# All 31 taps of the depthwise convolution of both channel halves on VectorE

## The chip, the cores and the metric

One NeuronCore of a Trainium2 chip. The metric is the device time of one launch in microseconds (us), the median of the timed runs. Engines are named as in the profile: PE is TensorE (matrix products and transposes), PEld its weight loads, DVE is VectorE, ACT is ScalarE, POOL is GpSimd.

## What is computed

Two layers of a first block and two layers of a second block run over 256 tokens of width 1024, in float32. The part that the change touches is a branch of the first block's mixer: 512 columns of a projection, gated to 256 channels, go through a causal depthwise convolution over 31 tokens, a layer norm, a SiLU and a small product.

```python
CONV_WIDTH, CONV_KERNEL = 256, 31

def conformer_conv(u, conv_dw, conv_b, ln_g, ln_b, conv_pw):
    a, g = jnp.split(u, 2, axis=-1)
    y = a * jax.nn.sigmoid(g)
    y = lax.conv_general_dilated(
        y, conv_dw[:, None, :], window_strides=(1,), padding=[(CONV_KERNEL - 1, 0)],
        dimension_numbers=('NWC', 'WIO', 'NWC'), feature_group_count=CONV_WIDTH)
    y = y + conv_b
    y = jax.nn.silu(layernorm(y, ln_g, ln_b))
    return jnp.einsum('bsc,cd->bsd', y, conv_pw)

# in each of the two layers of the first block:
#   y_attn = sparse attention (index scores, 64 best keys, softmax), 512 columns
#   y_conv = conformer_conv(...), 256 columns; y_pool = windowed means, 256 columns
#   h += rmsnorm(concat(y_attn, y_conv, y_pool) @ w_out); then feed forward and gate
```

## The kernel before

The 256 tokens are two halves of 128 (`t` = 0 and 1). Both halves run the same program, written as two generators; the second is held `LAG` = 4 steps behind the first, and each step is one load of weights: two planes of 128 rows by up to 512 columns (`cols`, line 115, or `rows`, line 137). The weights are loaded once and used by both halves. Each load is split exactly into two parts (`weights`, line 88): ScalarE rounds it to the high part (`whi`, line 101), VectorE subtracts to get the low part (`wlo`, line 102). Nine such pairs are kept (`SLOTS`). With inputs split in the same way, a product is three matmuls (`mm3`, lines 111 to 113): high by high, high by low, low by high. One load serves six matmuls for each half of the tokens. Sums go to two PSUM banks tagged `mm`, which ScalarE empties (`evac`, line 176); that step is moved forward in the scheduler's order by `URGENT`.

Small work that follows a product (transposes, rotary embedding at lines 395, 397 and 574, index scores at lines 584 to 592, selection of keys at lines 600 and 601, softmax) is hung behind later loads as chains of steps (`after`, `tick`). A scheduler then sets the order on each engine, once and for all: of the instructions that it takes to be ready, the one written first in the program goes first.

The convolution has channels on partitions: `conv_in[j]` holds channels 128 j to 128 j + 127 of all 256 tokens, with 30 zero columns ahead. When the second half of the tokens has filled it (`local_fill`), `pool_all` (the windowed means, lines 700 to 707, on VectorE) and `conv_all` are written. In `conv_all`, tap 0 with the bias is a ScalarE activation (line 729). Of channels 0 to 127, taps 1 to 26 are 26 ScalarE copies scaled by the tap (`part`, line 732, two buffers) that GpSimd adds up one after the other (line 733); taps 27 to 30 are summed on VectorE in `mine` (lines 745 and 747) and added by GpSimd (line 749). Of channels 128 to 255, taps 1 to 30 are 30 multiply-adds on VectorE (line 740), each of which reads the sum that the one before it wrote. `conv_finish` follows much later, ahead of the part of `w_out` that reads it.

Of the kernel before, what the change touches and what calls it, by code (L numbers as in the profile page):

```python
# [26 lines left out]
MP = 3  # L27
POOL_TAPS = (27, 1)
PARTS = 2
# [16 lines left out]
class Net:  # L46
# [15 lines left out]

# [1 line left out]
    def tile(self, shape, tag, dtype=F32, bufs=2, pool=None):  # L64
        return (pool or self.wk).tile(shape, dtype, tag=tag, name=tag, bufs=bufs)

    def mid(self, *shape):
        """A tile of up to 528 columns, shaped."""
        n = int(np.prod(shape))
        o = self.wk.tile([P, 528], F32, tag="mid", name="mid", bufs=MID)[:, :n]  # L70
        return o if len(shape) == 1 else self.shaped(o, shape)

    def small(self, *shape):
        """A tile of up to 320 columns, shaped."""
        n = int(np.prod(shape))
        o = self.wk.tile([P, 320], F32, tag="small", name="small", bufs=SMALL)[:, :n]
        return o if len(shape) == 1 else self.shaped(o, shape)
# [8 lines left out]

# [1 line left out]
    def weights(self, t, load):  # L88
        """The next two planes of weights in program order, [128, 2, width], as (hi, lo)."""
        i = self.pos[t]  # L90
        self.pos[t] += 1
        if t == 1:
            return self.cache.pop(i)
        nc = self.nc
        raw = self.raw_p.tile([P, 2, 512], F32, tag="raw", name="raw", bufs=RAW)
        hi = self.w_p.tile([P, 2, 512], F32R, tag="whi", name="whi", bufs=SLOTS)
        lo = self.w_p.tile([P, 2, 512], F32R, tag="wlo", name="wlo", bufs=SLOTS)
        width = load(raw)
        src = raw[:, :, :width]
        with self.tc.issue_after(self.last_act.ins) if i == 0 else nullcontext():  # L100
            nc.scalar.activation(hi[:, :, :width], src, AF.Copy)  # L101
        nc.vector.tensor_sub(lo[:, :, :width], src, hi[:, :, :width].bitcast(F32))  # L102
        self.cache[i] = hi, lo
        return hi, lo
# [10 lines left out]
    def cols(self, t, lhs, w, pieces, ps, ks=range(KD), first=True, last=True):  # L115
        """ps = x @ w[:, pieces], the pieces side by side; ks the rows' tiles."""
        ks = list(ks)
        width = sum(n for _, n in pieces)
        for c in range(0, len(ks), 2):
            k0 = ks[c]  # L120
# [16 lines left out]
    def rows(self, t, lhs, w, row0, nk, accs, first, last):  # L137
        """accs (two halves of 1024 columns) += x @ w[row0:row0 + 128 nk]."""
        for c in range(nk):
# [11 lines left out]

# [1 line left out]
    def after(self, t, steps, side=0):  # L153
# [17 lines left out]

# [1 line left out]
    def evac(self, out, ps, func, **k):  # L173
        """Empties a bank of products, before what the scheduler has pending."""
        with self.tc.high_priority(URGENT):
            self.nc.scalar.activation(out, ps, func, **k)  # L176
# [4 lines left out]
    def split(self, dst, k0, n, src):  # L181
        """src [128, 128 n] exactly as hi + lo at tiles k0.."""
        hi, lo = (d[:, k0:k0 + n, :] for d in dst)
        src = src.rearrange("p (k c) -> p k c", k=n)
        self.nc.scalar.activation(hi, src, AF.Copy)  # L185
        self.nc.vector.tensor_sub(lo, src, hi.bitcast(F32))
# [5 lines left out]
    def turn(self, dst, k0, n, src):  # L192
        """Tiles k0.. of dst = the transposed 128-column blocks of src, split."""
        ps = self.bank("tr")
        for j in range(n):
            self.transpose(ps, j, src[:, j * P:(j + 1) * P])
        self.split(dst, k0, n, ps[:, :n * P])
# [5 lines left out]
    def turn_scaled(self, src, vec, c0):  # L203
        """(src * vec)^T split, vec along the features."""
        nc = self.nc
# [14 lines left out]
    def rsqrt(self, sums, n, eps, half=False):  # L220
        """(sums / n + eps) ** -0.5 of one or several columns, or half of it; sums: the parts
        of the sums."""
        g = self.nc.gpsimd
# [54 lines left out]

# [1 line left out]
    def setup(self):  # L280
# [36 lines left out]
    def setup_late(self):  # L317
        nc, cp = self.nc, self.cp
        # in the room of what only the first block needed
        room = lambda tag, n: self.shaped(self.tile([P, n], tag, bufs=1)[:, :SEQ], (2, P))  # L320
# [8 lines left out]
        for l in range(2):  # L329
# [7 lines left out]
            nc.scalar.activation(e, e, AF.Exp)  # L337
            # ln(1 + e) with the rounding of 1 + e made good
            nc.vector.tensor_scalar(q, e, 1.0, None, op0=ALU.add)
# [17 lines left out]
    def rope_table(self, pos, freq, n, tag):  # L357
        """(cos, sin) of pos * freq, the angle brought to [-pi, pi] in three exact steps."""
        nc, cp = self.nc, self.cp
# [30 lines left out]
    def turned(self, a, b, x, table, n):  # L390
        """a = x cos, b = (second half, first half of x) (-sin, sin), in each of n heads."""
        v = self.nc.vector
# [5 lines left out]

# [1 line left out]
    def block1(self, t, l):  # L400
# [30 lines left out]

        # index queries and keys first, then the queries of the attention itself
        S = (t + 1) * P
# [91 lines left out]

        # feed forward
        x, r = self.pre_norm(t, vec, 8)
# [17 lines left out]

        # gate
        pe = self.small(256)
# [21 lines left out]
    def rotate(self, t, u, n):  # L569
        """Rotary embedding of the first 16 of every 64 columns, in place."""  # L570
        x = u.rearrange("p (h s d) -> p h s d", s=8, d=8)[:, :, 0:2, :]
# [4 lines left out]
    def score_index(self, t, jj, wi, qiT, kiT, idx, first):  # L576
        """idx += relu(qi ki) wi for the heads 4 jj .. 4 jj + 3."""
        nc = self.nc
# [16 lines left out]
    def select(self, t, idx):  # L595
        """idx = 0 at the 64 largest of those that may be seen, far below elsewhere."""
        nc = self.nc
# [63 lines left out]
    def local_start(self, t, l):  # L661
        """Room and weights for the convolution and the pool, of both halves of the tokens."""
        nc, io = self.nc, self.io
# [24 lines left out]
    def pool_all(self):  # L688
        """Windowed means less the input; the first 16 tokens see fewer."""
        v = self.nc.vector  # L690
# [31 lines left out]
    def conv_all(self, l):  # L722
        """Some of the taps on the vector engine, the others on the scalar engine and the Pool."""
        nc, vec = self.nc, self.v1[l]
# [59 lines left out]

# [1 line left out]
    def swiglu(self, t, l, name, c0):  # L786
# [27 lines left out]
    def gated(self, t, x, hr, w, name, accs, mix, then=None):  # L814
        """mix += (1 + tanh(gate / 2)) accs; the half of it comes at the end."""
        nc = self.nc
# [13 lines left out]
    def history(self, t, key, buf, n):  # L830
        """The n columns before buf's own: the other half's last, or none."""
        if t == 0:
# [5 lines left out]
    def features(self, s, nk, buf, k0, n):  # L838
        """buf[:, k0:k0 + nk, n:] = s^T."""
        tr = self.bank("tr")  # L840
# [5 lines left out]
    def mixer(self, t, l):  # L846
# [7 lines left out]

        # the recurrent branch's inputs between the heads of the retention
        ha, mix = [], []
# [54 lines left out]

        # short convolution
        bufs = [self.mid(4, 2 + P) for _ in range(2)]
# [59 lines left out]
    def block_diagonal(self, t, l, n, j):  # L973
        """Four 128-blocks, each of two 64-blocks of the gates' weights."""
        def make():
# [8 lines left out]
    def lru(self, t, l, j, s, out):  # L984
        """512 channels of the recurrent branch, twice over, appended to out."""
        nc = self.nc
# [30 lines left out]
        v = nc.vector  # L1017
        # half of log(a); a by its eighth root; 1 - a^2 = -tanh(log(a)) (1 + a^2)
        v.scalar_tensor_tensor(a, a, 1.0, lam[:, :, None].to_broadcast([P, 4, P]), op0=ALU.add, op1=ALU.mult)
# [63 lines left out]

# [1 line left out]
    def program(self, t, layers):  # L1085
# [46 lines left out]

# [1 line left out]
_BIG = ["w_in", "conv_pw", "pool_w", "w_out", "norm_mix_post", "w_up", "w_down", "norm_mlp_post",  # L1134
# [57 lines left out]
```

## Time and profile before

| | us |
|---|---|
| median of 3 timed runs | 2426.82 (2425.52 to 2427.87) |
| span of the profiled execution | 2426.7 |
| TensorE busy | 2361.9 |
| VectorE busy | 1570.9 |
| ScalarE busy | 1377.2 |
| GpSimd busy | 114.6 |

The two convolutions lie at about 50 to 90 us and 411 to 452 us of the span. A timeline row gives the start and the duration of an instruction, its engine, line and operation, what it writes and reads, and in brackets how long its engine stood still before it and what ended that. Instructions of an engine overlap a little: the step from one start to the next is what counts for its throughput. A windows row gives, for one stretch, the busy time of each engine with its instructions, the clock granted to TensorE as a share of 2.4 GHz, and the DMA traffic.

### The profile page before, as it was taken

How to read it: one execution, taken by the hardware profiler on the slowest of the kernel's cores; microseconds unless marked ns; L12 is line 12 of the kernel's file. 1: busy time of each engine (PE TensorE's matmuls, PEld its weight loads, DVE VectorE, ACT ScalarE, POOL GpSimd, SP SyncE). 2: the span in 40 equal slices, each digit the busy share in tenths (PEclk: the TensorE clock that was granted, in tenths of full speed). 3: DMA queues.
4: the chain of work that ended last, by engine and by line, in shares of the span. 5: the costliest groups of instructions: out<-in, count | busy, mean ns of one | idle time of the engine just before them, and what ended most of it. 6: DMA issues, size and time to landing. Idle time of an engine off the chain costs nothing.

```text
span 2426.7 us, 30886 instructions
## 1 busy us (share of the span) xinstructions
PE 2361.9 (97%) x10912; PEld 1913.5 (79%) x10912; DVE 1570.9 (65%) x2460; ACT 1377.2 (57%) x2137; POOL 114.6 (5%) x212
## 2 busy tenths in 40 slices
PE   7899998899999999999999999999999999999998
PEld 5678887678887887888788888878877888888887
DVE  5965566966566757766565665565587665656654
ACT  6655456655455757865455555555588554545543
POOL 1300002300000000000000000000000000000000
PEclk9899999999999999999999999999999999999999
DMA  6436554436556665555566665656655555666662
GB/s 188 139 100 195 187 158 140 139 108 194 189 174 193 190 185 159 155 179 172 175 189 194 188 192 184 190 182 187 186 161 160 171 170 174 193 197 190 184 189 87
DMA packets 264123, 417.90 MB, mean 172 GB/s; under 512 B 23712, under 2 KB 158624, under 8 KB 263968
## 3 DMA queue, kind: packets, MB, share of 16 engines
q1 hardware_dynamic: 261088, 414.26, 55.3%
q10 hardware_dynamic: 2880, 1.67, 0.2%
q8 instruction: 86, 1.41, 0.2%
q14 instruction: 69, 0.57, 0.1%
HBM read 414.81 MB, written 1.05 MB: 171 GB/s over the span
## 4 chain that ended last, share of the span: by engine, by line
PE 89%; DVE 5%; ACT 3%; issue 1%; POOL 1%; DMA 1%; SPq 0%; DVEq 0%; POOLq 0%; ACTq 0%
PE mm L111 19%; PE mm L113 18%; PE mm L112 18%; PE acc L111 9%; PE acc L112 9%; PE acc L113 9%; PE tr L179 4%; DVE wlo L102 1%; PE tr L1074 1%; DVE small L592 1%; POOL cvo L733 1%; ACT whi L101 1%; DVE cvo L740 1%; PE tr L1064 0%; PE tr L651 0%
## 5 line engine op out<-in xcount | busy, mean ns | idle before, releaser
L102 DVE TENSOR_TENSOR wlo<-raw,whi 128x1024 fp32r<-128x1024 f32 (+2 forms) x780 | 947.3, 1219 | 602.3 <-ACT whi L101 593.2
L101 ACT ACTIVATE whi<-raw 128x1024 fp32r<-128x1024 f32 (+2 forms) x780 | 817.3, 1052 | 656.2 <-PE mm L113 337.7
L111 PE MATMUL mm<-whi,xh 128*128 128x512 f32 (+2 forms) x2112 | 854.7, 405 | 20.1 <-ACT vv L176 8.9
L112 PE MATMUL mm<-wlo,xh 128*128 128x512 f32 (+2 forms) x2112 | 826.1, 392 | 8.1 <-DVE wlo L102 8.1
L113 PE MATMUL mm<-whi,xl 128*128 128x512 f32 (+2 forms) x2112 | 824.7, 392 | 1.3 <-DVE xl L216 1.3
L111 PEld LDWEIGHTS mm<-whi,xh 128*128 128x128 f32 x2112 | 401.4, 190 | 115.3 <-ACT vv L176 9.5
L112 PEld LDWEIGHTS mm<-wlo,xh 128*128 128x128 f32 x2112 | 402.0, 190 | 86.9 <-DVE wlo L102 11.0
L113 PEld LDWEIGHTS mm<-whi,xl 128*128 128x128 f32 x2112 | 400.9, 190 | 87.0 <-DVE xl L216 3.5
L111 PE MATMUL acc<-whi,mh 128*128 128x512 f32 x736 | 288.4, 392 | 0.9 <-ACT mh L185 0.8
L113 PE MATMUL acc<-whi,ml 128*128 128x512 f32 x736 | 287.5, 391 | 0.0
L112 PE MATMUL acc<-wlo,mh 128*128 128x512 f32 x736 | 286.9, 390 | 0.0
L111 PEld LDWEIGHTS acc<-whi,mh 128*128 128x128 f32 x736 | 138.2, 188 | 31.0 <-ACT mh L185 2.4
L112 PEld LDWEIGHTS acc<-wlo,mh 128*128 128x128 f32 x736 | 138.3, 188 | 29.2 <-DVE wlo L102 0.5
L113 PEld LDWEIGHTS acc<-whi,ml 128*128 128x128 f32 x736 | 138.2, 188 | 29.1
L111 PE MATMUL acc<-whi,xh 128*128 128x512 f32 x256 | 103.1, 404 | 2.3 <-ACT xh L185 2.2
L112 PE MATMUL acc<-wlo,xh 128*128 128x512 f32 x256 | 101.0, 396 | 0.0
L113 PE MATMUL acc<-whi,xl 128*128 128x512 f32 x256 | 100.6, 394 | 0.0
L185 ACT ACTIVATE mh<-tr 128x256 fp32r<-128x256 f32 (+1 forms) x140 | 62.9, 449 | 62.4 <-PE tr L179 62.4
L176 ACT ACTIVATE mid<-mm,rs_o 128x512 f32<-128x512 f32 (+2 forms) x112 | 74.3, 678 | 40.5 <-PE mm L113 40.1
L179 PE MATMUL tr<-ident,mid 128*128 128x128 f32 x504 | 78.6, 276 | 11.7 <-DVE mid L574 8.0
L176 ACT ACTIVATE small<-mm,hr 128x256 f32<-128x256 f32 x96 | 45.2, 474 | 74.6 <-PE mm L113 62.0
L179 PEld LDWEIGHTS tr<-ident,mid 128*128 128x128 f32 x504 | 61.7, 141 | 32.6 <-DVE mid L574 11.7
(227 smaller groups left out, 1767.1 us busy)
## 6 DMA issues: line engine op xcount, KB each, us to landing
raw<-ffn_w_in SPq DMA_DIRECT2D x352, 256.0 KB, 3.4
raw<-w_mix_in SPq DMA_DIRECT2D x160, 512.0 KB, 3.9
raw<-ffn_w_out SPq DMA_DIRECT2D x88, 512.0 KB, 3.7
raw<-w_up SPq DMA_DIRECT2D x64, 512.0 KB, 3.7
raw<-w_down SPq DMA_DIRECT2D x64, 512.0 KB, 3.7
raw<-w_mix_in SPq DMA_DIRECT2D x128, 256.0 KB, 3.1
raw<-w_ret_out SPq DMA_DIRECT2D x32, 512.0 KB, 3.7
raw<-w_in SPq DMA_DIRECT2D x24, 512.0 KB, 3.9
```

The costliest lines, as they stand in the source:

```text
L101: nc.scalar.activation(hi[:, :, :width], src, AF.Copy)
L102: nc.vector.tensor_sub(lo[:, :, :width], src, hi[:, :, :width].bitcast(F32))
L111: nc.tensor.matmul(o, xh[:, k, :], wh[:, j, :width], start=start, stop=False)
L112: nc.tensor.matmul(o, xh[:, k, :], wl[:, j, :width], start=False, stop=False)
L113: self.last[self.who] = nc.tensor.matmul(o, xl[:, k, :], wh[:, j, :width], start=False, stop=stop)
L176: self.nc.scalar.activation(out, ps, func, **k)
L179: self.nc.tensor.transpose(ps[:, j * P:(j + 1) * P], src, self.ident)
L185: self.nc.scalar.activation(hi, src, AF.Copy)
L592: nc.vector.scalar_tensor_tensor(idx, rl[:, i * S:(i + 1) * S], wi[:, hd:hd + 1], before, op0=ALU.mult, op1=ALU.add)
L733: nc.gpsimd.tensor_add(o, o, part)
L740: nc.vector.scalar_tensor_tensor(o, x[:, k:k + SEQ], w[:, k:k + 1], o, op0=ALU.mult, op1=ALU.add)
L1074: nc.tensor.matmul(po, sT[:, i, :], self.shared[("rv", l, hd, t - i)], start=(i == 0), stop=(i == t))
```

## The change

`POOL_TAPS` says how many taps of each half of the channels go by way of ScalarE and GpSimd, tap 0 included. It goes from (27, 1) to (1, 1). With 1, the loop over lines 731 to 733 is empty and the branch of line 738 takes taps 1 to 30, so both halves of the channels run as 30 multiply-adds of line 740 in place; the tiles `part` and `mine` of the convolution are not used. All else in the diff is comments.

```diff
-POOL_TAPS = (27, 1)
+POOL_TAPS = (1, 1)
```

## Rows read from the trace of the kernel before

**Rows 1.** The page: busy time, share and instructions of each engine.
```profile
PE 2361.9 (97%) x10912; PEld 1913.5 (79%) x10912; DVE 1570.9 (65%) x2460; ACT 1377.2 (57%) x2137; POOL 114.6 (5%) x212
```
**Rows 2.** Busy time by stretch (us), first layer; PEclk is the granted clock.
```profile
57.60:62.00 4.40, 0.00 (x0) 0.00 (x0) 4.40 (x7) 4.01 (x10) 3.73 (x6) 0.87 0.00 0
62.00:75.00 13.00, 9.00 (x21) 5.64 (x22) 13.00 (x20) 8.44 (x16) 10.78 (x11) 0.52 0.36 98
75.00:90.00 15.00, 13.70 (x67) 10.19 (x66) 14.44 (x30) 10.44 (x19) 8.07 (x8) 1.00 0.28 92
90.00:115.00 25.00, 22.34 (x123) 16.31 (x121) 24.34 (x74) 12.04 (x23) 0.74 (x2) 1.00 0.62 197
115.00:160.00 45.00, 40.32 (x220) 30.90 (x220) 33.85 (x101) 23.94 (x65) 2.62 (x5) 0.96 0.31 96
```
**Rows 3.** The same view, columns PE, PEld, DVE, ACT, POOL, second layer.
```profile
418.90:423.30 4.40, 0.00 (x0) 0.00 (x0) 4.40 (x7) 4.02 (x10) 3.72 (x6) 0.93 0.01 2
```
**Rows 4.** Timeline of TensorE, first layer: start, duration, engine, line, operation.
```profile
62.05 0.80 PE L111 MATMUL mm<-whi,xh 128*128 128x512 f32 x1 [4.45 <-ACT vv L176]
...
70.62 0.79 PE L112 MATMUL mm<-wlo,xh 128*128 128x512 f32 x1 [1.16 <-DVE wlo L102]
...
74.37 0.46 PE L112 MATMUL mm<-wlo,xh 128*128 128x512 f32 x1
74.67 0.39 PE L113 MATMUL mm<-whi,xl 128*128 128x512 f32 x1
74.90 0.39 PE L111 MATMUL mm<-whi,xh 128*128 128x512 f32 x1
```
**Rows 5.** Timeline of ScalarE, first layer.
```profile
47.59 1.06 ACT L101 ACTIVATE whi<-raw 128x1024 fp32r<-128x1024 f32 x1
...
55.56 0.51 ACT L732 ACTIVATE part<-cvi,v 128x256 f32<-128x256 f32 x1 [2.78 <-POOL cvo L733]
...
61.65 0.35 ACT L176 ACTIVATE vv<-mm,rs_o 128x128 f32<-128x128 f32 x1
```
**Rows 6.** The convolution's sum: instructions, durations (ns, min/median/max), first and last start.
```profile
L740 DVE SCALAR_TENSOR_TENSOR cvo<-cvi,v,cvo x60: 468/476/1011, 53.6 to 451.3; 128x256 f32<-128x256 f32 x60
L733 POOL TENSOR_TENSOR cvo<-cvo,part x52: 722/821/3220, 51.4 to 445.1; 128x256 f32<-128x256 f32 x52
```
**Rows 7.** Timeline of VectorE, first layer.
```profile
50.78 0.34 DVE L745 TENSOR_SCALAR mine<-cvi,v 128x256 f32<-128x256 f32 x1
...
54.05 0.47 DVE L747 SCALAR_TENSOR_TENSOR mine<-cvi,v,mine 128x256 f32<-128x256 f32 x1
54.45 0.47 DVE L740 SCALAR_TENSOR_TENSOR cvo<-cvi,v,cvo 128x256 f32<-128x256 f32 x1
56.37 0.35 DVE L592 SCALAR_TENSOR_TENSOR small<-mid,wi,causal 128x128 f32<-128x128 f32 x1 [1.45 <-ACT mid L588]
...
61.99 1.75 DVE L102 TENSOR_TENSOR wlo<-raw,whi 128x1024 fp32r<-128x1024 f32 x1
...
64.53 0.78 DVE L395 TENSOR_TENSOR ro_a<-mid,ra0c 128x96 f32<-128x96 f32 x1
...
93.39 0.26 DVE L395 TENSOR_TENSOR ro_a<-mid,ra1c 128x96 f32<-128x96 f32 x1
```
**Rows 8.** VectorE's groups by form, 50.7 to 90.5 us: busy us, mean ns, idle.
```profile
L740 DVE SCALAR_TENSOR_TENSOR cvo<-cvi,v,cvo 128x256 f32<-128x256 f32 x30 | 19.2, 641 | 0.0
L102 DVE TENSOR_TENSOR wlo<-raw,whi 128x1024 fp32r<-128x1024 f32 x5 | 7.7, 1534 | 0.0
L592 DVE SCALAR_TENSOR_TENSOR small<-mid,wi,small 128x128 f32<-128x128 f32 x7 | 3.8, 544 | 0.6 <-ACT mid L588 0.6
```
**Rows 9.** The same view of VectorE over the whole span.
```profile
L102 DVE TENSOR_TENSOR wlo<-raw,whi 128x1024 fp32r<-128x1024 f32 x764 | 935.3, 1228 | 594.6 <-ACT whi L101 585.5 <-DMA raw<-ffn_w_in 4.4 <-DMA small<-freq 0.6
```
**Rows 10.** Windows, 57.6 to 78.8 us: line 113 alone, then all lines.
```profile
57.60:78.80 21.20, 4.25 (x9) 2.34 (x9) 0.68 0.26 75
57.60:78.80 21.20, 12.80 (x41) 8.51 (x42) 21.20 (x35) 15.08 (x29) 16.44 (x17) 0.68 0.26 75
```

## Prediction

> **What bounds the kernel now.** I read the table of engines first: TensorE is busy for 97% of the span, VectorE for 65%, ScalarE for 57%, GpSimd for 5% [rows 1]. Seen over the whole span, VectorE has room for more work. But the change touches one short stretch in each of two layers, so I then read the stretches by windows, and there the order is another. From 57.6 to 62.0 us TensorE does nothing at all while VectorE is busy throughout; from 62 to 75 TensorE is busy for 9.0 us of 13, at a granted clock of 0.52 (the lower of its two levels, 1.2 GHz, nearly all the time), and VectorE is full; only from 75 on does TensorE run well, with 1.3 us idle to 90, 2.7 to 115 and 4.7 to 160 [rows 2]. The second layer repeats the hole at 418.9 [rows 3]. So the kernel is bound by TensorE nearly everywhere, and by the queues of VectorE and ScalarE in two stretches of some 60 us. What the change is worth is decided there. It can reach no other stage: the convolution runs once in each of the two layers.
>
> Next, what opens the hole. TensorE's product at 62.05 waited 4.45 us for an eviction (line 176) [rows 4]. That eviction sat in ScalarE's queue behind scaled copies (line 732) that waited for GpSimd, one of them 2.78 us, and ran at 61.65 only [rows 5]. GpSimd's adds take 0.82 us at the median and 3.2 at most, where a tap on VectorE takes 0.476 [rows 6]. Then TensorE waits for VectorE: for the low part of the next weights (line 102) [rows 4]. Its high part was ready at 48.65 (47.59 + 1.06) [rows 5], yet VectorE took it up at 61.99 [rows 7]: pooling, taps and index scores went ahead of it. That order is the heart of this prediction.
>
> **What the change does, part by part.** Only POOL_TAPS acts; the rest of the diff is comments. For each layer:
>
> *Removed from ScalarE and GpSimd:* 26 scaled copies and 27 adds. The evictions then run when their bank is full. The 4.45 us wait goes.
>
> *Added to VectorE:* 30 multiply-adds for channels 0 to 127, less the four that were there (lines 745 and 747): 26 net. Two taps of different chains follow each other by 0.40 us (54.05 to 54.45) although each lasts 0.47 [rows 7]. 26 x 0.40 = +10.4 us. Bounds: 0.40 if the two chains alternate, 0.476 if each waits for its end [rows 6], which gives 12.4. The two chains are independent, so I take 0.40.
>
> *Given back on VectorE:* work beside GpSimd's adds is slow. Between 50.7 and 90.5 the 30 taps average 641 ns [rows 8] against 476 [rows 6]: 30 x 0.165 = 5.0 us. Five weight splits average 1534 [rows 8] against 1228 over the run [rows 9]: 1.5. Seven index scores 544 [rows 8] against 351 for one alone [rows 7]: 1.4. Some seven small rotary and pooling instructions lose 0.5 each, as the one at 64.53 (0.78) shows against the same shape at 93.39 (0.26) [rows 7]: 3.6. Sum 11.5 us. VectorE also stood still for 1.45 us at 54.9 [rows 7] and 0.56 between 75 and 90 [rows 2], both behind ScalarE: 2.0. So VectorE's load to the end of this stretch is 10.4 - 11.5 - 2.0 = -3.1 us. Twenty-six more instructions cost VectorE nothing in sum.
>
> The Trainium skill (SBUF — State Buffer, "Who interferes with whom") says that a VectorE instruction with two SBUF inputs and a GpSimd instruction that reads SBUF lock each other out for the whole instruction. By that, each of 26 adds could hold VectorE for up to 0.82 us, 21.3 in sum, and the load would fall by 12.9 us instead of 3.1. The trace agrees that there is a loss but shows about 0.5 us for a hindered instruction [rows 7, 8], so my sum keeps 11.5.
>
> *Moved: the order on VectorE.* One chain of taps leaves a gap between a tap and the next that needs it, and the trace fills each gap with one other instruction: a weight split, a rotary step, an index score. Where two chains were ready (52.3 to 54.9) they filled each other's gaps, and the split that had been ready since 48.65 got none [rows 5, 7]. After the change two chains of 30 run side by side all the way. So I expect a block: taps begin at 50.8, and 60 x 0.40 = 24.0. From 50.78 to 54.85 six taps ran (four of one chain, two of the other, 2.3 us), so the other 1.8 were pooling, 1.4 unhindered, and they stay [rows 7]: the block ends near 76.2. Behind it wait four index scores and four rotary steps (durations of 0.35 and 0.26, some 1.7 by their starts) [rows 7], then the next split, 1.2 [rows 9]: TensorE gets its weights at about 79, where before it got them at 63.7 (61.99 + 1.75).
>
> *What TensorE has until then.* It runs dry at 57.6. With evictions prompt, the second half of the tokens can take its next column from four weight parts that are already split: 24 products of 0.23 us, by their step at full clock [rows 4], 5.5 us. Before, in 57.6 to 78.8, it did 9 triples, 27 products (6.2 us at full clock), and 14 transposes and scores (1.7), spread thin and slow [rows 10]: 7.9 us of work. So at 78.8 it is 2.4 us behind, not 15. The cover is those four parts; without it the lag is 7.9.
>
> *Restart.* After the long idle the clock stands at 1.2 GHz. In the last unbroken run before it rose, TensorE worked from 70.62 to 74.37 at that level [rows 4]: half of 3.75 us lost, 1.9 (bounds 0, if work before keeps the clock up, and 4.3, half of what 62 to 75 lost at 0.52 [rows 2]). I take 1.9.
>
> *Given back later.* Once the block is over, ScalarE has prepared many high parts, VectorE needs 1.2 us for a split that feeds TensorE for 2 x 6 x 0.23 = 2.8, and TensorE can use the idle time it had before: 1.3 + 2.7 to 115, 4.7 to 160 [rows 2]. Bounds 0 and 8.6. Chains (scores, selection, softmax) keep the last part, so I take half of the first two: 2.0.
>
> Sum for a layer: 2.4 + 1.9 - 2.0 = +2.3; two layers +4.6. The profiled span is 2426.7 and the median 2426.82, so nothing lies between. Prediction 2431.5 us.
>
> **The rivals.**
> 1. *VectorE's queue sets the end (faster).* VectorE is full from 60 to 115 (24.3 of 25 us after 90) [rows 2]. If that queue, not weights, decides when attention ends, each layer ends 3.1 us earlier: 2420.6. It decides from the point where TensorE recovers over 4.3 us of its 8.6 idle. For it: the load falls. Against it: its order puts what TensorE needs last.
> 2. *The splits slip in between (faster).* If the taps don't close up, weights come as before or earlier, the 4.45 us and part of the slow clock go: 5 us a layer, 2417. Against it: 52.3 to 54.9.
> 3. *No cover (slower).* If TensorE's own order puts a product that needs the late split ahead of the ready column, it stands from 57.6 to 78.8: 7.9 + 1.9 = 9.8 a layer less what is given back, about 2442 to 2446.
> 4. *Nothing moves.* The block's lag is wholly eaten by later idle: 2427. The Trainium skill (Perfetto Trace Analysis, "Identifying the Most-Contended Engine") says that a kernel improves by its most contended engine; by that, shifting work among the others at 97% TensorE [rows 1] would leave 2427 as it is. The windows speak against it here, since in the stretch the full engine is VectorE [rows 2].
> That the change does nothing is out: with 1 in place of 27, line 740's branch takes the taps of both halves.
>
> **How the numbers follow.** A measurement of this kernel tells about 0.2% (4.9 us) from no change. Block with cover, +0.7 (more given back) to +5 a layer (nothing given back, a dearer restart), 2428 to 2437: 0.45, of which 0.26 lies above +4.9. Rival 1: 0.20, half beyond -4.9. Rival 2: 0.08, all faster. Rival 3: 0.19, all slower. Rival 4: 0.08. Faster 0.18, same 0.37, slower 0.45. The range leaves out the far half of rivals 2 and 3: 2417 to 2444. Cases of both signs are within it; the forecast's own range is 2428 to 2437.
>
> **What would show it.** Right: no GpSimd adds; taps of both chains alternating 0.40 us apart without other work between, over 24 us; taps at 0.47 throughout; no long wait for line 176; one TensorE hole, about 63 to 78 us and 424 to 440, that ends on line 102; clock at 0.5 for some 4 us after it. Wrong: a split among the taps (rival 2), a hole from 57.6 (rival 3), or a TensorE with hardly any idle from 79 to 160 and a VectorE free some 3 us earlier (rival 1).

## The result and the profile after

The changed kernel took 2440.45 us (median of 4 runs, 2439.23 to 2440.68); the kernel before, run beside it on the same chip, 2427.35 (4 runs, 2425.52 to 2428.04). The ratio is 1.0059, with a 95% interval of 1.0047 to 1.0071: 13.1 us slower, 6.5 a layer. The profiled span is 2438.5 us. Forecast were 2431.5 us: the direction was right, the loss is nearly three times the 4.6 us of the sum, outside the forecast's own range (2428 to 2437) and just under the 2442 to 2446 of rival 3. Tap 0 of each half, with the bias, is still a ScalarE activation (line 729), so 30 of the 31 taps are VectorE's.

The table of engines after (to be held against [rows 1]), and the convolution's sum (against [rows 6]; durations in ns, min/median/max):

```profile
PE 2354.0 (97%) x10912; PEld 1911.1 (78%) x10912; DVE 1573.5 (65%) x2512; ACT 1356.3 (56%) x2085; POOL 56.9 (2%) x158
L740 DVE SCALAR_TENSOR_TENSOR cvo<-cvi,v,cvo x120: 466/468/474, 49.9 to 442.5; 128x256 f32<-128x256 f32 x120
```

VectorE has 52 more instructions and only 2.6 us more to do. Every tap takes 0.47 us now, none 1.0. The load is near what the prediction had; the order is what is to be seen next. VectorE's timeline, first layer (start, duration, what ran; a count closes the row):

```profile
47.94 1.21 DVE L102 TENSOR_TENSOR wlo<-raw,whi 128x1024 fp32r<-128x1024 f32 x1
...
51.65 22.24 DVE L740 SCALAR_TENSOR_TENSOR cvo<-cvi,v,cvo 128x256 f32<-128x256 f32 x56
73.81 0.33 DVE L592 SCALAR_TENSOR_TENSOR small<-mid,wi,causal 128x128 f32<-128x128 f32 x1
...
74.73 0.24 DVE L395 TENSOR_TENSOR ro_a<-mid,ra0c 128x96 f32<-128x96 f32 x1
...
75.66 1.21 DVE L102 TENSOR_TENSOR wlo<-raw,whi 128x1024 fp32r<-128x1024 f32 x1
```

56 taps stand in one unbroken block of 22.2 us. Behind it wait the first index score, which ran at 56.37 before [rows 7], the first rotary step (64.53 before [rows 7]) and the next weight split. TensorE, with what ended its idle time in brackets, first and second layer:

```profile
56.23 0.39 PE L111 MATMUL mm<-whi,xh 128*128 128x512 f32 x1
76.93 0.80 PE L112 MATMUL mm<-wlo,xh 128*128 128x512 f32 x1 [20.31 <-DVE wlo L102]
...
445.34 0.79 PE L112 MATMUL mm<-wlo,xh 128*128 128x512 f32 x1 [20.28 <-DVE wlo L102]
```

One hole of 20.3 us in each layer, which ends on line 102, where before there were 4.45 us and several short waits [rows 4]. ScalarE's queue shows what else stood still:

```profile
78.40 0.37 ACT L453 COPY mid<-tr 128x256 f32<-128x256 f32 x1 [22.57 <-PE tr L179]
78.67 0.53 ACT L176 ACTIVATE mid<-mm,rs_o 128x320 f32<-128x320 f32 x1
```

Line 453 waits for transposes, these for the rotary step behind the block, and an eviction stands in ScalarE's queue behind line 453. So all three engines wait for VectorE's taps.

The windows after (busy time of PE, PEld, DVE, ACT, POOL, then the granted clock; against [rows 2]):

```profile
56.60:76.90 20.30, 0.02 (x1) 0.00 (x0) 20.30 (x54) 0.00 (x0) 0.00 (x0) 0.62 0.00 0
76.90:84.00 7.10, 7.07 (x26) 5.05 (x26) 5.22 (x15) 2.31 (x6) 0.00 (x0) 0.64 0.76 231
84.00:90.00 6.00, 6.00 (x29) 4.53 (x30) 5.21 (x10) 3.18 (x7) 0.00 (x0) 1.00 0.62 202
90.00:115.00 25.00, 23.10 (x124) 17.69 (x122) 21.22 (x66) 14.58 (x26) 0.00 (x0) 1.00 0.48 160
115.00:160.00 45.00, 41.43 (x235) 31.78 (x234) 33.19 (x100) 24.25 (x63) 3.35 (x7) 1.00 0.29 99
```

After the hole TensorE works for 7.07 us at a mean clock of 0.64, so 72% of it, 5.1 us, at 1.2 GHz: 2.6 us lost. From 90 to 160 it is idle for 5.5 us against 7.3 before [rows 2], but the stretches don't hold the same work: the thin one at the end, with its slow clock, lies within 160 us before and behind it after. The windows, before and then after:

```profile
156.00:160.00 4.00, 3.27 (x9) 2.35 (x10) 2.35 (x5) 0.68 (x3) 0.00 (x0) 0.57 0.02 6
```
```profile
160.00:164.00 4.00, 3.03 (x9) 2.04 (x8) 2.51 (x4) 0.84 (x2) 0.00 (x0) 0.57 0.04 16
```

The waits of TensorE over the whole run (us in total, times, longest), after and then before:

```profile
PE mm L112 <- DVE wlo L102: 43.6, 4, 20.3
PE tr L179 <- DVE mid L574: 3.7, 2, 1.9
```
```profile
PE mm L111 <- ACT vv L176: 8.9, 2, 4.5
PE mm L112 <- DVE wlo L102: 8.1, 6, 3.2
PE tr L179 <- DVE mid L574: 8.0, 8, 1.9
```

Splits +35.5, evictions -8.9, rotary steps -4.3: +22.3. All of TensorE's idle time grew by 19.7 (span less busy, 84.5 against 64.8; the other 2.6 lie in small waits), its busy time fell by 7.9: +11.8, which is the difference of the two spans. Part of the fall is less work at the slow clock: 5.1 us after the hole, where nearly all of the 9.0 us from 62 to 75 were slow before [rows 2].

### The profile page after: what moved, and what is told of

Same layout as the page of the kernel before. It is cut to its first block, busy times and chain, and to the rows that moved or that the text cites. A ratio compares the mean times of both kernels' runs of the same rounds, so it can differ in the third digit from the quotient of the medians.

```text
span 2438.5 us, 30803 instructions
## 1 busy us (share of the span) xinstructions
PE 2354.0 (97%) x10912; PEld 1911.1 (78%) x10912; DVE 1573.5 (65%) x2512; ACT 1356.3 (56%) x2085; POOL 56.9 (2%) x158
## 4 chain that ended last, share of the span: by engine, by line
PE 89%; DVE 5%; ACT 3%; DMA 1%; issue 1%; POOL 0%; SPq 0%; DVEq 0%; ACTq 0%; POOLq 0%
PE mm L111 19%; PE mm L113 18%; PE mm L112 18%; PE acc L111 9%; PE acc L113 9%; PE acc L112 9%; PE tr L179 4%; DVE cvo L740 2%; PE tr L1074 1%; DVE wlo L102 1%; ACT whi L101 1%; PE tr L651 0%; DVE small L592 0%; PE tr L617 0%; PE tr L1064 0%
## 5 line engine op out<-in xcount | busy, mean ns | idle before, releaser
L112 PEld LDWEIGHTS acc<-wlo,mh 128*128 128x128 f32 x736 | 138.3, 188 | 29.1 <-DVE wlo L102 0.5
L113 PEld LDWEIGHTS acc<-whi,ml 128*128 128x128 f32 x736 | 138.2, 188 | 29.1
```

The costliest lines, as they stand in the source:

```text
L112: nc.tensor.matmul(o, xh[:, k, :], wl[:, j, :width], start=False, stop=False)
L113: self.last[self.who] = nc.tensor.matmul(o, xl[:, k, :], wh[:, j, :width], start=False, stop=stop)
```

## The experiments

Each was timed beside the kernel before on the same chip, and differences are against that. In one session were: one chain, portions of both chains, half the taps as one chain, the cover; in the next: portions of one chain, half the taps as two chains, and the two without the adds; then the two with splits first; then the last two. Line numbers shift by a few in the edited kernels.

**One chain.** The taps of channels 128 to 255 are issued after those of 0 to 127, nothing else.

```
+    with self.tc.issue_after(tap.ins) if j else nullcontext():
+        for k in rest:
-    for k in rest:
-        nc.vector.scalar_tensor_tensor(o, x[:, k:k + SEQ], w[:, k:k + 1], o, op0=ALU.mult, op1=ALU.add)
+            tap = nc.vector.scalar_tensor_tensor(o, x[:, k:k + SEQ], w[:, k:k + 1], o, op0=ALU.mult, op1=ALU.add)
```

> The changed kernel with one more rule of order: the 30 taps of channels 128 to 255 are issued after the 30 of channels 0 to 127, so that the taps are one chain of 60 in place of two side by side. The same instructions, on the same engines. Theory 'order' (the loss of some 7 us a layer is TensorE waiting for weight splits behind an unbroken block of 56 taps): each tap again leaves a gap that one other instruction fills, the first late split comes before 60 us, the 20.3 us wait of TensorE is gone, and the time falls to 2412 to 2427. Rival 'work' (26 more instructions for each layer on a VectorE that is full there): the time stays at 2436 to 2441.

2424.34 us (10 runs) against 2426.29: ratio 0.9996 [0.9987, 1.0005]. The whole loss is gone with the same instructions in another order. TensorE still has a hole that ends on a split, but it is half as long and later (10.8 us, ending at 96.6). VectorE's timeline in this kernel, first layer, shows taps that alternate with what else is ready:

```profile
52.28 0.34 DVE L592 SCALAR_TENSOR_TENSOR small<-mid,wi,causal 128x128 f32<-128x128 f32 x1
...
53.95 0.47 DVE L741 SCALAR_TENSOR_TENSOR cvo<-cvi,v,cvo 128x256 f32<-128x256 f32 x1
54.34 0.34 DVE L592 SCALAR_TENSOR_TENSOR small<-mid,wi,small 128x128 f32<-128x128 f32 x1
54.61 0.47 DVE L741 SCALAR_TENSOR_TENSOR cvo<-cvi,v,cvo 128x256 f32<-128x256 f32 x1
55.00 1.21 DVE L102 TENSOR_TENSOR wlo<-raw,whi 128x1024 fp32r<-128x1024 f32 x1
```

**Portions of both chains.** conv_all is a generator that the second half's steps advance; it gives out three taps of each chain at a time.

```
-            self.conv_all(l)
+            self.after(t, self.conv_all(l), 1)
...
+PER = 3
...
+            if k % PER == 0:
+                yield
```

> The changed kernel with the taps written in ten portions of three pairs, one portion with each of ten later steps of the second half of the tokens, in place of all at once. The same work. 'Order': splits that are written between the portions go ahead of the later portions; the long wait of TensorE falls to under 6 us and the time to 2412 to 2425. 'Work': 2436 to 2441.

2420.72 us (10 runs): 0.9979 [0.9970, 0.9988]. Order again, here with both chains side by side within a portion.

**Portions of one chain.** The same, six taps of a single chain at a time.

> The changed kernel with the taps in ten portions as in the run with pairs, but each portion six taps of one chain (first channels 0 to 127, then 128 to 255), so that a gap is left behind each tap as well. 'Order' allows a little more than the pairs gave (2420.7), since no portion can close up: 2415 to 2421. If VectorE's load in the stretch is what is left as the bound, no difference: 2419 to 2424.

2417.65 us (9 runs) against 2426.97: 0.9965 [0.9955, 0.9974], 9.3 us under the kernel before and the fastest of the kernels with the whole convolution. In places taps of the one chain stood next to each other too, at the same step as in the block (VectorE's timeline):

```profile
63.23 2.06 DVE L739 SCALAR_TENSOR_TENSOR cvo<-cvi,v,cvo 128x256 f32<-128x256 f32 x5
```

So the gap behind each tap of one chain is the scheduler's order and nothing that VectorE needs.

**Half the taps, as one chain and as two.** The first leaves out taps 1 to 30 of channels 0 to 127, by the diff; the second leaves out taps 16 to 30 of all channels, by a range that ends at 16: the same number of taps, of the same cost.

```
-            rest = range(POOL_TAPS[j], CONV_K)
+            rest = range(POOL_TAPS[j], CONV_K) if j else []
```

> The changed kernel without taps 1 to 30 of channels 0 to 127 (left out). One chain of 30 taps remains for each layer, with no work on GpSimd. 'Order': no block, every tap followed by other work; with neither GpSimd's adds nor a block it ends below the kernel before, at 2400 to 2418, and shows the floor for this stretch. 'Work': the time falls by the 30 taps that are gone, 12 us a layer at most, 2416 to 2440.

> The changed kernel with taps 1 to 15 in each chain (taps 16 to 30 of both left out): 30 taps for each layer, as many as in the run with one half's taps left out (2397), but as two chains side by side. 'Order': the block shrinks by 30 x 0.40 = 12 us to some 12 us, TensorE's wait from 20.3 to about 8 us, and the time lands between, at 2408 to 2420; the distance to 2397 is the price of the block for equal work. 'Work': 2393 to 2401, as with one chain.

One chain: 2397.22 us (4 runs), 29.1 under the kernel before, 0.9876 [0.9859, 0.9892], below both expected ranges. Two chains: 2416.89 (5 runs), 10.1 under, 0.9960 [0.9946, 0.9974]. For equal work the block costs 19.0 us. TensorE's waits for splits over the run (us in total, times, longest), one chain first, then two:

```profile
PE mm L112 <- DVE wlo L102: 3.0, 2, 2.3
```
```profile
PE mm L112 <- DVE wlo L102: 20.6, 4, 8.5
```

Against the changed kernel, two chains of 15 have 30 taps a layer less; the long wait fell from 20.3 to 8.4 us in the first layer, 11.9, about 30 x 0.40. And with one chain, 60 more taps (30 more a layer) cost 2424.34 - 2397.22 = 27.1 us, 0.45 each: almost a tap's duration.

**What the old path cost.** The kernel before without GpSimd's adds (lines 733, 749; the diff), and without the adds and the 26 scaled copies a layer (line 732 too).

```
                 part = self.tile([P, SEQ], "part", bufs=PARTS)
                 nc.scalar.activation(part, x[:, k:k + SEQ], AF.Copy, scale=w[:, k:k + 1])
-                nc.gpsimd.tensor_add(o, o, part)
...
-                nc.gpsimd.tensor_add(o, o, mine)
```

> The kernel before without GpSimd's adds (left out; ScalarE's copies stay, and 34 taps a layer stay on VectorE). From the chain of 60 (2424) and the chain of 30 (2397) a tap costs (2424.3 - 2397.2) / 60 = 0.45 us. If GpSimd's adds are what the kernel before paid for, through VectorE's slow instructions and ScalarE's wait for the two buffers, the time is 2397 + 8 x 0.45 = 2401, up to 2408 with the copies' own time: 18 to 26 us less than before. If the copies on ScalarE are the cost, it stays above 2418.

> The kernel before without GpSimd's adds and without ScalarE's 26 scaled copies a layer (both left out). Against the run without the adds alone this prices the copies: 0 to 4 us if ScalarE has room for them (57% busy), 8 to 20 if evictions wait behind them.

2415.50 us (4 runs), 11.5 under the kernel before, 0.9956 [0.9941, 0.9970]: between the two bands. 2397.68 (4 runs), 29.3 under, 0.9881 [0.9867, 0.9896]. Without the adds the copies no longer wait for GpSimd and run together, ahead of the eviction, so the two numbers can't be read as the price of adds and of copies apart. ScalarE's timeline without the adds, first layer:

```profile
48.10 10.50 ACT L732 ACTIVATE part<-cvi,v 128x256 f32<-128x256 f32 x26
...
59.98 0.37 ACT L176 ACTIVATE vv<-mm,rs_o 128x128 f32<-128x128 f32 x1
```

Together they can: the path through ScalarE and GpSimd cost 29.3 us, and the 52 taps that replace it cost at 0.45 about 23. By these prices the change is worth about 6 us in a good order: the run with one chain got 2.0, the portions 5.6 and 9.3, the last more than the sum allows.

**The cover.** The first half of the tokens is held back after the convolution until the second half has done eight more steps, so that its next column comes first.

```
+            self.hold = self.done[0] + AHEAD, self.done[1] + 8
...
-                if not live[t] or (t == 1 and live[0] and done[0] - done[1] <= LAG):
+                held = self.hold and done[0] >= self.hold[0] and done[1] < self.hold[1]
+                if not live[t] or (t == 0 and held) or (
+                        t == 1 and live[0] and done[0] - done[1] <= LAG and not held):
```

> The changed kernel with the first half of the tokens held at its step until the second half has written its next column, for which four weight parts are already split when the block of taps begins. The block of taps stays. If the missing cover is what separates the prediction (+2.3 us a layer) from the result (+7), TensorE has 24 more products to do in the hole, the wait of 20.3 us shrinks by about 5.5 us, and the time falls by 5 to 11 us, to 2429 to 2435. If idle time later on swallows what the cover gives, it stays at 2437 to 2441.

2452.75 us (4 runs): 1.0109 [1.0094, 1.0124], slower than both expectations. TensorE's timeline in this kernel: the products ran, the last at 62.19, and a hole of 17 us followed them:

```profile
62.19 0.39 PE L116 MATMUL mm<-whi,xl 128*128 128x512 f32 x1
79.76 0.90 PE L182 MATMUL tr<-ident,mid 128*128 128x128 f32 x3 [17.18 <-DVE mid L489]
...
87.32 0.79 PE L114 MATMUL mm<-whi,xh 128*128 128x512 f32 x1 [3.75 <-ACT vv L179]
```

The edit also changed the order in which the steps of the two halves are written there, and a wait for an eviction followed (3.75 us), so its price isn't that of the cover alone. But it raised a doubt that the next four runs pursue: TensorE now waited for a copy that follows a rotary step (line 489), not for a split.

**What may stand behind the block.** In the changed kernel (two chains of 30) the next eight splits get the evictions' priority and so a place ahead of the block.

```
+        with self.tc.high_priority(URGENT) if self.soon >= 0 else nullcontext():
             nc.vector.tensor_sub(lo[:, :, :width], src, hi[:, :, :width].bitcast(F32))
```

> The taps and their two chains stay as in the changed kernel; only the next eight weight splits after the convolution is issued get the priority that the evictions have, so that four of them instead of one stand ahead of the block of taps on VectorE (the block itself stays, 50 taps or so in a row). If the lateness of the splits is what costs: three more early splits take 3 x 1.2 us of VectorE and feed TensorE for 3 x 2.8 us, so the hole shrinks from 20.3 us to about 16 and each layer gains some 4.8 us: 2429 to 2434. If VectorE's load sets the end of the stretch, order is worth nothing: 2438 to 2442.

2443.29 us (4 runs) against 2424.02: 1.0077 [1.0061, 1.0092], no faster than the change as it was. Five splits ran between 46 and 58 us, and then a block of 48 taps. In TensorE's timeline the hole is as long as after the change alone, under another name:

```profile
59.95 0.39 PE L117 MATMUL mm<-whi,xl 128*128 128x512 f32 x1
80.51 0.90 PE L183 MATMUL tr<-ident,mid 128*128 128x128 f32 x3 [20.17 <-DVE mid L578]
```

The same edit on top of the portions of one chain, for the next 24 splits in place of eight:

> The taps in ten portions of one chain each, as in the run with portions, and the splits of the stretch with the priority of the evictions. If late splits are still what costs there (13.7 us of waits of TensorE for splits in that run), these waits fall to 5 us or less and the time from 2417.7 to 2405 to 2411. If only VectorE's work is left to pay, the same number of instructions gives 2415 to 2420; above 2420 if something else that the splits overtake (rotary steps, index scores) becomes the late one.

2433.25 us (6 runs): 1.0030 [1.0017, 1.0044]. It took away the waits for splits (13.7 us in the run with portions) and brought others, 21.4 us for rotary steps; against the portions alone it lost 18.5 us (9.2 over the kernel before instead of 9.3 under). Early splits alone don't help, then. So the next six rotary steps and groups of index scores got the priority instead, with the splits left behind the block (a line of the same kind stands ahead of the index scores):

```
+        with self.tc.high_priority(URGENT) if self.steps >= 0 else nullcontext():
             self.turned(a, b, x, self.rope1[t], n)
             self.nc.vector.tensor_add(x, a, b)
```

> The changed kernel with its two chains of taps; only the rotary and index-score steps that follow the convolution get the evictions' priority, so that on VectorE the first score group and two rotary steps stand among the first dozen taps, and a block of some 38 taps follows, with the next splits behind it. The run with early splits left the hole at 20.2 us, with a rotary step as the late one. If the steps of the attention are what must not be late, and splits matter little: 2420 to 2428. If the block costs by itself, whatever TensorE asks for next standing behind it: a hole of 14 to 20 us that ends on a split, and 2434 to 2443.

2422.95 us (10 runs) against 2425.30: 0.9988 [0.9979, 0.9998]. The loss is gone although TensorE still has a hole of 10.7 us, and VectorE's timeline a block of 38 taps with the next split behind it:

```profile
58.61 15.11 DVE L747 SCALAR_TENSOR_TENSOR cvo<-cvi,v,cvo 128x256 f32<-128x256 f32 x38
...
74.85 1.21 DVE L104 TENSOR_TENSOR wlo<-raw,whi 128x1024 fp32r<-128x1024 f32 x1
```

Then both in front:

> The same with the next eight splits in front as well: scores, rotary steps and four splits stand before or among the first taps, and a block of 50 taps follows. If late steps of either kind were the cause and both are now early: 2412 to 2425. If the block costs by itself: the hole only moves to the first step that still stands behind it (a copy of the keys, the next split), 15 to 20 us long, and 2434 to 2443.

2436.23 us (4 runs): 1.0043 [1.0028, 1.0058], with a hole of 12.0 us. Splits in front of the block cost 13.3 us even when the attention's steps are in front too. The first index score did not move by much (3.7 us behind the last fill of the convolution's input, 3.1 without the splits), but 50 taps and not 38 stood in the block, which ended 31.0 us behind the fill and not 26.9.

**What these runs did to TensorE.** None of the edits moved one thing alone. The windows from the last fill of the convolution's input (first layer) to the instruction behind the hole, products into the banks `mm` alone, give the time to the hole's end, TensorE's busy time, the number of products and the clock; in order the change as it was, splits first, attention first, both first:

```profile
47.14:76.93 29.79, 8.90 (x43) 0.74 0.07 19
47.85:80.51 32.66, 11.91 (x56) 0.76 0.25 81
46.81:74.58 27.77, 15.21 (x67) 0.87 0.08 24
51.20:83.09 31.89, 18.21 (x80) 0.87 0.25 83
```

Splits first gave TensorE 13 products more, some 3.0 us at 0.23, but its hole ended 2.9 us later: nothing won (the traced executions took 2440.04 us and, in the change as it was, 2440.34). Attention first gave it 24 more, 5.5 us, and ended the hole 2.0 us earlier: 7.5 a layer, where 7.7 were measured (from +6.5 to -1.2). Both first doesn't fit this account: 37 more, 8.5 us, less 2.1 would win 6.4 a layer, and 1.1 were measured. Nor does the cover, with 60 products and a hole that ended after 31.3 us.

**One yardstick for all.** The steps of the attention form a chain, and its end may be what sets the layer's. I took from each trace, in the first layer, the time from the last fill of the convolution's input (ScalarE, line 682 in the kernel before) to the last maximum over the attention's scores (VectorE, line 621). The two rows of the timelines, in the kernel before and then after:

```profile
49.98 0.45 ACT L682 COPY cvi<-tr 128x128 f32<-128x128 f32 x2
142.90 0.08 DVE L621 DVE_READ_ACCUMULATOR2_ANT mx<- 128x1 f32 x1
```
```profile
47.14 0.44 ACT L682 COPY cvi<-tr 128x128 f32<-128x128 f32 x2
147.40 0.08 DVE L621 DVE_READ_ACCUMULATOR2_ANT mx<- 128x1 f32 x1
```

| kernel | fill to last maximum, us | against before | second layer, against before | time against before, per layer |
|---|---|---|---|---|
| before | 92.9 | | | |
| after | 100.3 | +7.4 | +8.0 | +6.5 |
| one chain | 91.3 | -1.6 | -0.1 | -1.0 |
| portions of both chains | 89.6 | -3.3 | -4.0 | -2.8 |
| portions of one chain | 91.9 | -1.0 | -5.5 | -4.7 |
| half the taps, one chain | 77.9 | -15.0 | -16.2 | -14.5 |
| half the taps, two chains | 89.9 | -3.0 | -3.9 | -5.0 |
| without adds | 87.5 | -5.4 | -4.9 | -5.7 |
| without adds and copies | 78.9 | -14.0 | -13.9 | -14.6 |
| cover | 104.7 | +11.8 | +12.9 | +13.2 |
| splits first | 99.9 | +7.0 | +7.5 | +9.6 |
| portions, splits first | 96.6 | +3.7 | +3.6 | +4.6 |
| attention first | 91.8 | -1.1 | -0.2 | -1.2 |
| both first | 96.7 | +3.8 | +2.9 | +5.5 |

Over a range of 28 us a layer the first layer's difference agrees with the time within 3.7 and the mean of both layers within 2.4. That they move together doesn't prove which one leads: the stretch holds TensorE's hole too, and whatever delays TensorE there delays its end. TensorE's longest hole orders the runs less well: 17.2 us in the cover, the slowest, against 20.3 in the change as it was, and 7.6 with portions and splits first (2433.25 us) against 10.7 with the attention first (2422.95).

## Why the prediction came out as it did

*Load: right.* The 26 more taps a layer add 52 x 0.40 = 20.8 us to VectorE's busy time by their step (24.3 by their full duration of 0.468), and it grew by 2.6. So 18.2 to 21.7 us of hindrance went, 9.1 to 10.9 a layer, where the sum had 11.5. The rule of the Trainium skill that two such instructions lock each other out entirely (SBUF — State Buffer, "Who interferes with whom") gave 21.3 a layer as its bound; the trace supports about half of that.

*Block: right.* Predicted 24.0 us at 0.40 a tap, ending near 76.2; 56 taps took 22.24 and the block ended at 73.9 (one split slipped in ahead of it, at 47.94). The fill came 2.8 us earlier in this execution (47.14 against 49.98), so counted from it the end lies within 0.6 us of the forecast's. The sum's upper bound of 0.476 for taps that wait for each other has no support: taps of one chain stepped by 0.40 too. Rival 2 fell. The wait for line 176 went, as predicted.

*Cover: the step that failed first.* It was to give TensorE 24 products before the hole, so that the lag was 2.4 us and not 7.9. The trace shows none of it: TensorE did the six products of the split that ran ahead of the block (from 54.74), then the first product of the late one, at 56.23, and stood. Counted from the fill, the hole opened after 9.5 us; rival 3's place (57.6) is 7.6, the forecast's (63) 13. What the sum had for TensorE before the hole, 24 products, was there in no layer.

*Rival 3 is what the trace shows.* Its condition is met, a product of the late split ahead of the ready column, and so is its price. Counted through TensorE's instructions in order, each from its kernel's fill, the 245th starts 9.8 us later than before (9.1 for the same place in the second layer), where rival 3 had 7.9 + 1.9; at the 560th 7.3 are left (8.0). The direction came out right because the block and the restart were right; the forecast's 2431.5 lay too low because its cover was missing, and the result's place near 2442 is rival 3's.

*What remains open is why the order costs what it does.* One account is TensorE's: too few products ahead of the hole. It fits splits first and attention first and misses both first by 5.3 us a layer; the cover came out slower where it would have been faster. The other is the attention's chain on VectorE: its first index score moved from 6.4 us after the fill (56.37 - 49.98) to 26.7 (73.81 - 47.14), and by its end 7.4 us of those 20.3 were left. It is argued from the yardstick and not shown, since every run that moved the chain also moved the hole; and with splits first the first rotary step came 31.4 us behind the fill and not 27.6, with no later last maximum. Rival 1 had named VectorE's queue as what decides when attention ends, but counted its load (-3.1) and not its order.

*Restart and what is given back.* Restart was 1.9, measured 2.6. Given back, by the count just told, were 2.5 us in the first layer (9.8 - 7.3) and 1.1 in the second, against 2.0 predicted. Both were of the right size. The clock gave nothing back: its 1.00 from 115 to 160 (0.96 before [rows 2]) only means that the slow spell came at 160 to 164.

*Rival 4* fell, and with it the rule of the Trainium skill (Perfetto Trace Analysis, "Identifying the Most-Contended Engine") as rival 4 applied it, to the whole span: TensorE is at 96 to 98%, none of the edits gave it more or less to do, and the kernels with the whole convolution still lie between 2417.7 and 2452.8 us. The trace speaks against that use here, as the windows had it [rows 2].

What stays open besides: what a cover without other changes is worth, why splits in front cost 13.3 us when the attention's steps are in front too, and how the 29.3 us of the old path divide between copies and adds.

## To carry to other kernels

In the scheduler's order two independent chains of equal priority filled each other's gaps and made a block of 56, while one chain left a gap after each link for whatever was ready: before moving work to an engine, write down what will stand behind it there, and issue it as one chain or in portions. The wait that the profile names at the end of a hole is only the first thing behind the block; moving it ahead handed the hole to the next (20.31 us for a split became 20.17 for a rotary step), so look at all that stands behind the block; here the attention's chain was what paid to put first. An engine's share of the span (65% here) says little: in this stretch 60 more taps cost 0.45 us each, nearly all of their 0.47.

## What the runs showed of the hardware beside this

Taps on VectorE step by 0.40 us (22.24 / 56) although each shows 0.468: the end of one overlaps the start of the next. That holds for taps of one chain too, where each reads the sum that the one before wrote (five in 2.06 us). A scaled copy of 128x256 on ScalarE steps by 0.40 too when nothing holds it (10.50 / 26), while GpSimd's add of the same shape took 0.82 [rows 6]. So a tap done by ScalarE and GpSimd took three times the engine time (0.40 + 0.82) of one done by VectorE alone, and held VectorE up besides.
